# A short first load from adjacent rows, both first loads ahead of the barrier, and a transposed store

## The chip, the cores and the metric

One core of one Trainium2 chip; the other cores are idle. The metric is the device time of one execution in microseconds. The span of a profile runs from the first to the last instruction of the kernel and is some 1.3 us shorter. Where engines start, land or carry packets, the 16 DMA engines are meant.

## The reference

```python
x = np.random.randn(32, 512, 1024).astype(np.float32)   # 67.1 MB
relu_x = np.maximum(x, 0)
return np.sum(relu_x, axis=-1)                           # 32 x 512 sums
```

## The kernel before

The 16384 rows are dealt to 128 partitions. Region 0 gives each partition 112 neighbouring rows, region 1 gives it 16. Region 0 is loaded in seven chunks of 16 rows (64 KB per partition, one packet each; 16 DMA engines with 8 packets each) into three buffers; region 1 in ever smaller pieces, so that little work is left after the last landing. ScalarE takes the ReLU, VectorE the sums. SyncE issues all transfers. The first load's instruction is moved ahead of the barrier with which all engines open the program.

```python
REGIONS = [112, 16]
CHUNKS = [(0, 0), (0, 16), (0, 32), (0, 48), (0, 64), (0, 80), (0, 96)]
TAIL = [8, 4, 2, 1]
LAST = [512, 256, 256]
# ... views, buffers, semaphores cut ...
    for c in range(NBIG + 1):
        if c >= NB:
            sp.wait_ge(s_dve, done[c - NB])        # the buffer is free
        if c < NBIG:
            g, j = CHUNKS[c]
            sp.dma_start(out=buf[:, c % NB, :, :], in_=xv[g][:, j : j + BIG, :]).then_inc(
                s_in[c], 16
            )
        if c == 0:
            code.insert(arrival, code.pop())       # ahead of the barrier
# ... tail loads cut ...
    sp.wait_ge(s_fact, 1)
    sp.wait_ge(s_fdve, 1)
    for g in range(len(REGIONS) - 1):              # sums of region 0
        sp.dma_start(out=ov[g][:, :], in_=res[:, start[g] : start[g] + REGIONS[g]]
        ).then_inc(s_store, 16)
# ... ReLU on ScalarE, sums on VectorE, per chunk, cut ...
    sp.wait_ge(s_tdve, 1)
    sp.dma_start(out=ov[-1][:, :], in_=res[:, start[-1] : J]).then_inc(s_out, 16)
    sp.wait_ge(s_store, 16 * (len(REGIONS) - 1))
    sp.wait_ge(s_out, 16)
```

## Time and profile before

| | before |
|---|---|
| time, median of 3 runs | 161.12 us (161.08 to 161.19) |
| span of the profiled run | 159.8 us |
| first chunk taken up by ScalarE | 21.84 us |
| distance of the later chunks | 19.36 us (433 GB/s) |
| from the last load's landing to the end | 2.0 us |

How to read it: the time that ScalarE's first instruction of a chunk starts is the landing of that chunk plus 0.02 us, as long as "DMA" stands behind its idle time. A chunk has landed when the slowest of the 16 engines has landed its eight packets. So these few starts show the whole flow: the first one the start, their distances the rate. The lines are in the prediction below.

### The profile page before, as it was taken

The page shows a single profiled execution, that of the slowest core. Times are in us where ns is not written, and L with a number is a line of the kernel's source. Part 1 is how long each engine was busy: PE and PEld are TensorE (multiplying, and loading weights), DVE is VectorE, ACT ScalarE, POOL GpSimd, SP SyncE. Part 2 cuts the span into 40 slices and gives each one's busy share as a digit, 9 for nine tenths or more (in the row PEclk, how much of TensorE's full clock was granted, in tenths as well). Part 3 has the DMA queues.
Part 4 walks back from the last instruction along what each step waited for, and adds up shares of the span by engine and source line. Part 5 has one row for each costly group of instructions (what it writes and reads, how often), then busy time and mean ns, then how long its engine had stood idle before and what let it go on. Part 6 is the DMA issues. An engine that isn't in the chain of part 4 may idle for free.

```text
span 159.8 us, 148 instructions
## 1 busy us (share of the span) xinstructions
DVE 121.4 (76%) x58; ACT 101.5 (63%) x55; POOL 0.2 (0%) x4
## 2 busy tenths in 40 slices
DVE  0000000999959999999969989699899999598995
ACT  3000059990699808996099951999339980496974
POOL 0000000000000000000000000000000000000000
DMA  7996996996997998989969969969969969899994
GB/s 262 525 525 262 525 525 262 525 525 262 525 443 344 525 410 377 525 361 427 525 295 492 525 279 509 525 262 525 525 262 525 525 262 525 353 435 394 406 393 138
DMA packets 2305, 67.18 MB, mean 420 GB/s; under 512 B 512, under 2 KB 768, under 8 KB 1024
## 3 DMA queue, kind: packets, MB, share of 16 engines
q1 hardware_dynamic: 2304, 67.18, 98.0%
q14 instruction: 1, 0.01, 0.0%
HBM read 67.11 MB, written 0.07 MB: 420 GB/s over the span
## 4 chain that ended last, share of the span: by engine, by line
DMA 68%; ACT 18%; DVE 11%; SPq 1%; issue 0%
DMA buf<-in_x_dram 68%; ACT buf L130 18%; DVE res L145 11%; SPq L92 1%; SPq L100 0%; DVE buf L115 0%; DVE last L115 0%
## 5 line engine op out<-in xcount | busy, mean ns | idle before, releaser
L145 DVE TENSOR_REDUCE res<-buf 128x7 f32<-128x7168 f32 (+4 forms) x17 | 100.1, 5923 | 34.0 <-ACT buf L130 34.0
L130 ACT ACTIVATE buf<-buf 128x7168 f32<-128x7168 f32 (+4 forms) x16 | 80.7, 5099 | 46.5 <-DMA buf<-in_x_dram 46.5
L112 ACT ACTIVATE buf<-buf 128x1024 f32<-128x1024 f32 (+1 forms) x19 | 19.0, 1000 | 9.0 <-DMA buf<-in_x_dram 8.9
L115 DVE TENSOR_SCALAR_CACHE_REDUCE buf<-buf 128x1024 f32<-128x1024 f32 (+2 forms) x19 | 20.9, 1146 | 2.8 <-DMA buf<-in_x_dram 2.5
L112 ACT ACTIVATION_READ_ACCUMULATOR buf<-buf 128x1 f32 x19 | 3.5, 186 | 0.0
L130 ACT ACT_TABLE_LOAD x1 | 1.3, 1283 | 0.8 <-PEq L206 0.8
L115 DVE DVE_READ_ACCUMULATOR buf<-buf 128x1 f32 x19 | 1.6, 83 | 0.0
L115 DVE TENSOR_SCALAR_CACHE_REDUCE last<-last 128x258 f32<-128x258 f32 x1 | 0.4, 422 | 0.0
L175 DVE TENSOR_TENSOR res<-half 128x1 f32<-128x1 f32 x1 | 0.2, 160 | 0.1
L206 POOL MEMSET const-bfloat16-1.0<- 128x1 bf16 x1 | 0.1, 101 | 0.0
L206 POOL MEMSET const-uint8-127<- 128x1 uint8 x1 | 0.1, 101 | 0.0
L206 POOL MEMSET const-float32-0.0<- 128x1 f32 x1 | 0.1, 98 | 0.2 <-issue 0.2
L206 POOL MEMSET const-float32-1.0<- 128x1 f32 x1 | 0.1, 98 | 0.0
L115 DVE DVE_READ_ACCUMULATOR last<-last 128x1 f32 x1 | 0.1, 81 | 0.0
## 6 DMA issues: line engine op xcount, KB each, us to landing
buf<-in_x_dram SPq DMA_DIRECT2D x1, 4096.0 KB, 26.7
buf<-in_x_dram SPq DMA_DIRECT2D x1, 2048.0 KB, 31.2
buf<-in_x_dram SPq DMA_DIRECT2D x1, 1024.0 KB, 33.2
buf<-in_x_dram SPq DMA_DIRECT2D x1, 512.0 KB, 34.0
buf<-in_x_dram SPq DMA_DIRECT2D x1, 256.0 KB, 34.2
buf<-in_x_dram SPq DMA_DIRECT2D x1, 128.0 KB, 34.1
last<-in_x_dram SPq DMA_DIRECT2D x1, 128.0 KB, 34.0
buf<-in_x_dram SPq DMA_DIRECT2D x7, 36.3
```

What stands on the lines that cost most here:

```text
L92: sp.dma_start(out=buf[:, tb, r : r + n, :], in_=xv[-1][:, r : r + n, :]).then_inc(s_in[NBIG + i], 16)
L112: return act.activation(t, t, AF.Relu, accum_out=acc)
L115: return dve.tensor_scalar(out=t, in0=t, scalar1=0.0, scalar2=None, op0=ALU.max, op1=ALU.add, accum_out=acc)
L130: act.activation(t, t, AF.Relu).then_inc(s_act, 1)
L145: dve.tensor_reduce(out=res[:, c * BIG + r : c * BIG + r + n], in_=buf[:, c % NB, r : r + n, :], axis=X, op=ALU.add,).then_inc(s_dve, 1)
L175: dve.tensor_tensor(out=res[:, j0 + r : j0 + r + 1], in0=half[:, 0:1], in1=half[:, 1:2], op=ALU.add)
L206: nc = _bacc.Bacc("TRN2", target_bir_lowering=False, num_devices=1)
```

## The change

Intent: let the engines get going on short packets (4 KB) from 128 adjacent rows before they turn to packets of 60 KB, with both parts of the first chunk issued at once, and so begin the flow earlier. The row of the first region has one sum per partition. To store 128 sums of 4 bytes as four pieces of 128 bytes, VectorE transposes 32 x 32 blocks of them.

```diff
-REGIONS = [112, 16]
-CHUNKS = [(0, 0), (0, 16), (0, 32), (0, 48), (0, 64), (0, 80), (0, 96)]
+REGIONS = [1, 111, 16]
+CHUNKS = [[(0, 0, 1), (1, 0, 15)]] + [[(1, 16 * c + 15, 16)] for c in range(6)]
-DVE_STEPS = [[7, 9], [7, 4, 5], ...cut
+DVE_STEPS = [[7, 9], [7, 9], ...cut
@@ loads
-            g, j = CHUNKS[c]
-            sp.dma_start(out=buf[:, c % NB, :, :], in_=xv[g][:, j : j + BIG, :]).then_inc(s_in[c], 16)
-        if c == 0:
-            code.insert(arrival, code.pop())
+            i = 0
+            for g, j, n in CHUNKS[c]:
+                sp.dma_start(
+                    out=buf[:, c % NB, i : i + n, :], in_=xv[g][:, j : j + n, :]
+                ).then_inc(s_in[c], 16)
+                i += n
+                if c == 0:
+                    code.insert(arrival, code.pop())
+                    arrival += 1
@@ stores
-    for g in range(len(REGIONS) - 1): ...cut
+    sp.dma_start(out=ov[1][:, :], in_=res[:, start[1] : start[2]]).then_inc(s_store, 16)
+    sp.wait_ge(s_turn, 1)
+    sp.dma_start(
+        out=of[0:P].rearrange("(k q) -> k q", q=32), in_=turned[0:P:32, 0:32]
+    ).then_inc(s_store, 16)
@@ waits of ScalarE and VectorE
-        act.wait_ge(s_in[c], 16)
+        act.wait_ge(s_in[c], 16 * len(CHUNKS[c]))
@@ VectorE, behind the sums of chunk 1
+        if c == 1:
+            dve.wait_ge(s_dve, done[c])
+            dve.transpose(out=turned[:, :], in_=res[:, 0:32]).then_inc(s_turn, 1)
```

More of the change, by code (lines that the diff above doesn't have):

```diff
@@ L7 @@
 NB = 3
-REGIONS = [112, 16]
-CHUNKS = [(0, 0), (0, 16), (0, 32), (0, 48), (0, 64), (0, 80), (0, 96)]
+REGIONS = [1, 111, 16]
+CHUNKS = [[(0, 0, 1), (1, 0, 15)]] + [[(1, 16 * c + 15, 16)] for c in range(6)]
 ACT_STEPS = [[7, 9], [7, 9], [4, 5, 7], [4, 5, 7], [4, 5, 7], [3, 4, 5]]
-DVE_STEPS = [[7, 9], [7, 4, 5], [4, 5, 7], [4, 5, 7], [4, 5, 7], [3, 4, 5]]
+DVE_STEPS = [[7, 9], [7, 9], [4, 5, 7], [4, 5, 7], [4, 5, 7], [3, 4, 5]]
 TAIL = [8, 4, 2, 1]
@@ L50, in bass_relu_sum_kernel @@
     res = nc.alloc_sbuf_tensor("res", [P, J], fp32)
+    turned = nc.alloc_sbuf_tensor("turned", [P, 32], fp32)
     n_in = NBIG + len(TAIL) + len(LAST)
@@ L60, in bass_relu_sum_kernel @@
     s_tdve = nc.alloc_semaphore("s_tdve")
+    s_turn = nc.alloc_semaphore("s_turn")
     s_store = nc.alloc_semaphore("s_store")
@@ L82, in bass_relu_sum_kernel @@
         if c < NBIG:
-            g, j = CHUNKS[c]
-            sp.dma_start(out=buf[:, c % NB, :, :], in_=xv[g][:, j : j + BIG, :]).then_inc(
-                s_in[c], 16
-            )
-        if c == 0:
-            code.insert(arrival, code.pop())
+            i = 0
[7 more added lines that the diff above has]
+                    arrival += 1
     r = 0
@@ L104, in bass_relu_sum_kernel @@
     sp.wait_ge(s_fdve, 1)
-    for g in range(len(REGIONS) - 1):
-        sp.dma_start(
-            out=ov[g][:, :], in_=res[:, start[g] : start[g] + REGIONS[g]]
-        ).then_inc(s_store, 16)
+    sp.dma_start(out=ov[1][:, :], in_=res[:, start[1] : start[2]]).then_inc(s_store, 16)
[3 more added lines that the diff above has]
+    ).then_inc(s_store, 16)
     def on_act(t, acc):
@@ L136, in bass_relu_sum_kernel @@
         if alone:
-            dve.wait_ge(s_in[c], 16)
+            dve.wait_ge(s_in[c], 16 * len(CHUNKS[c]))
             for i in range(BIG - alone, BIG - alone // 2):
@@ L151, in bass_relu_sum_kernel @@
             r += n
+        if c == 1:
+            dve.wait_ge(s_dve, done[c])
+            dve.transpose(out=turned[:, :], in_=res[:, 0:32]).then_inc(s_turn, 1)
     j0 = NBIG * BIG
     for c in range(NTWO, NBIG):
-        act.wait_ge(s_in[c], 16)
-        dve.wait_ge(s_in[c], 16)
+        act.wait_ge(s_in[c], 16 * len(CHUNKS[c]))
+        dve.wait_ge(s_in[c], 16 * len(CHUNKS[c]))
         for i in range(BIG):
```

## The prediction

> **What bounds the kernel now.** I read the page first for the busy shares and the packets, then the timeline for the moments at which loads land, then windows over the first microseconds, because the change touches little but the start, and last the chain and the wait list for the end.
>
> ```profile
> span 159.8 us, 148 instructions
> DVE 121.4 (76%) x58; ACT 101.5 (63%) x55; POOL 0.2 (0%) x4
> ...
> q1 hardware_dynamic: 2304, 67.18, 98.0%
> ```
>
> The load queue is busy for 98% of what 16 engines have in the span; VectorE (76%) and ScalarE (63%) both have room. The timeline, columns start, length, engine, line, operation, with the idle time before it in brackets, says the same about ScalarE, which takes each chunk when it lands:
>
> ```profile
> 0.79 1.28 ACT L130 ACT_TABLE_LOAD   x1 [0.79 <-PEq L206]
> 21.84 13.95 ACT L130 ACTIVATE buf<-buf 128x7168 f32<-128x7168 f32 x2 [19.77 <-DMA buf<-in_x_dram]
> ...
> 41.20 13.95 ACT L130 ACTIVATE buf<-buf 128x7168 f32<-128x7168 f32 x2 [5.41 <-DMA buf<-in_x_dram]
> ...
> 118.60 10.63 ACT L130 ACTIVATE buf<-buf 128x3072 f32<-128x3072 f32 x3 [5.31 <-DMA buf<-in_x_dram]
> ...
> 137.96 1.06 ACT L112 ACTIVATE buf<-buf 128x1024 f32<-128x1024 f32 x1 [6.65 <-DMA buf<-in_x_dram]
> ...
> 147.66 1.06 ACT L112 ACTIVATE buf<-buf 128x1024 f32<-128x1024 f32 x1 [1.28 <-DMA buf<-in_x_dram]
> ```
>
> Chunks arrive every 41.20 - 21.84 = 19.36 us, from the second to the seventh alike (118.60 to 137.96 is 19.36 again). A chunk is 16 rows of 128 x 4 KB = 8.389 MB, so the flow is 433 GB/s. The first tail piece, 8 rows, takes 147.66 - 137.96 = 9.70 us, 1.21 us per row, and 19.36 / 16 is 1.21 too. The input is 128 such rows: 128 x 1.21 = 154.9 us of the 159.8 us. What is left is a start of some 21.84 - 19.36 = 2.48 us, from the first issue to the moment from which the flow counts (its landing latency included), and an end of some 2 us after the last landing. So only about 4.5 us of the span can be touched at all without a faster flow, and 2% of the time would be 3.2 us.
>
> The windows split the start. Columns: window, length, busy times of three engines, clock, DMA share, GB/s. A packet counts in the window in which it starts, with its whole length and size, so shares over 1 are no error.
>
> ```profile
> 0.00:1.00 1.00, 0.00 (x0) 0.21 (x1) 0.20 (x4) 1.00 0.00 0
> 1.00:2.00 1.00, 0.00 (x0) 1.00 (x1) 0.00 (x0) 1.00 3.09 1049
> 2.00:3.00 1.00, 0.00 (x0) 0.07 (x1) 0.00 (x0) 1.00 0.00 0
> 3.00:4.00 1.00, 0.00 (x0) 0.00 (x0) 0.00 (x0) 1.00 0.00 0
> 4.00:5.00 1.00, 0.00 (x0) 0.00 (x0) 0.00 (x0) 1.00 2.42 1049
> ```
>
> 1049 GB/s for 1 us is 16 packets of 64 KB, one per engine. The first 16 begin between 1 and 2 us and last 3.09 us on average; the second 16 last 2.42 us, which is the pace of the whole stream (65,536 B in 2.42 us is 27.1 GB/s, times 16 again 433). So the first packet of each engine costs 0.67 us more than later ones. Narrower windows:
>
> ```profile
> 1.00:1.10 0.10, 0.00 (x0) 0.10 (x1) 0.00 (x0) 1.00 14.33 4588
> ...
> 1.70:1.90 0.20, 0.00 (x0) 0.20 (x1) 0.00 (x0) 1.00 0.82 328
> ...
> 4.06:4.25 0.19, 0.00 (x0) 0.00 (x0) 0.00 (x0) 1.00 4.75 2059
> 4.25:4.40 0.15, 0.00 (x0) 0.00 (x0) 0.00 (x0) 1.00 4.03 1748
> 4.40:4.53 0.13, 0.00 (x0) 0.00 (x0) 0.00 (x0) 1.00 6.98 3025
> ```
>
> 4588 x 0.10 / 65.5 is 7 engines that begin in the first tenth; one begins only after 1.70. The share of the early seven is 14.33 x 0.10 x 16 / 7 = 3.28 us each, that of the late one 0.82 x 0.20 x 16 = 2.62. The engines that began first thus paid 0.86 us extra, the one that began last 0.20. The second packets start between 4.06 and 4.53; less 2.42 this is an "effective start" of 1.64 for the best engine and 2.11 for the worst. All engines carry equal bytes, so the worst one ends the stream.
>
> **What the Trainium skill says.** (1) "Perfetto Trace Analysis", section on the HWDGE DMA instruction: the profiled time of an issue leaves out the data movement, and an engine may begin before all descriptors are made. The trace agrees: the first issue is at 0.00, data begins 1.00 us later. (2) "DMA: Bandwidth & Descriptors", "Where 436 GB/s comes from": a ceiling of 435.2 GB/s at the SBUF ports. The trace has 433, so the flow itself has nothing to give. (3) The same page, "Latency and other measured facts", on HBM row pitch: large power-of-two pitches between partitions lose bandwidth, with streams in lock step as an unverified reason. Here the pitch is 112 x 4 KB = 448 KB; the steady stream loses nothing by it, and only the slow first packets would fit. (4) "VectorE: DVE Perf Modes", "The three transpose paths": VectorE transposes separate 32x32 blocks, 311 ns for 128x128 in bf16. No transpose is in the trace before.
>
> **The change part by part.**
>
> *The first load in two.* Row 0 of each partition now comes from 128 adjacent rows (512 KB in one piece), then 15 rows at a pitch of 111 x 4 KB = 444 KB. Removed: the first 64 KB packet on scattered addresses, all engines at once. Each engine instead starts with 8 packets of 4 KB, close together. If the extra 0.67 us is the engines getting in each other's way on far-apart addresses, the worst effective start falls from 2.11 towards the bound that the late engine shows (it began after 1.70 and paid 0.20: about 2.0), or towards 1.2 to 1.5 for early engines, if the late ones were late for the same reason. I take 1.75, a gain of 0.36 us; it is my choice between 2.0 and 1.5. Added: one more transfer boundary per engine. From the landings, 19.36 against 8 x 2.415 of data is 0.04 us per boundary; short packets add about as much again (4 KB in eight packets against one of 32 KB), so 0.08 us. Net -0.28 us.
>
> *Both loads ahead of the barrier.* An issue takes some 0.4 us, so SyncE comes to the barrier about 0.4 us later and ACT_TABLE_LOAD moves from 0.79 to about 1.2. ScalarE then idles 19.77 us before its first work: 0 on the path. Loads two and three are issued 0.4 us later, twenty and forty microseconds ahead of need: 0. The 15-row issue comes 0.4 us after the first, which holds 8 x 0.15 = 1.2 us of work per engine: no hole. ScalarE still waits for both parts, so no computing starts earlier.
>
> *VectorE.* In chunk 1 the 4-row and 5-row sums (4.42 + 5.48 us by the rows of section 5) become one of 9 rows (9.75): -0.15 us. The wait on itself and one transpose add an estimated 0.3 us. Chunk 1 ends at 65.0, and the load that waits for it is queued behind one that lands at 79.9: 15 us of slack, 0 on the path.
>
> *The stores.* One more issue (0.35 us) at about 147.6, four packets of 128 B, behind the loads. The first store is issued at 147.26 and lands 10.7 us later, 157.96; the last one goes out at 158.33 and lands 1.4 us later. Loads were all issued by 124.2. So the added store is finished with the first one: 0.
>
> Sum: 161.12 - 0.36 + 0.08 = 160.84; rounded, 160.8 us.
>
> **The rivals.** *The start is bound by the arming of the rings.* Then the late engine starts as late as now, the slowest effective start stays about 2.0 to 2.1, the boundary eats the rest: 161.1 to 161.2. For it: the engine that began last paid almost nothing extra and was still among the slow ones. Against: the early ones lost most, so something shared held them. *The 444 KB pitch slows the flow.* Each 1% of the 135 us of region 1 would be 1.3 us. Against it: 448 KB (chunks) and 64 KB (tail, 1.21 us per row) run at the same pace, set at the engines. It would need over 2% to matter. *The late barrier or the added store is on the path:* +0.4 us, 161.5. Against it are the 19.77 us of idle time and the store's slack. *A larger gain:* all engines at full pace from 1.2 us, 0.9 us less 0.08: 160.3. That would also need the late engines to start early.
>
> **Range and chances.** The range runs from most of the larger gain (160.3) to slightly above no gain at all (161.25). Beyond 2% on the fast side would need 3.2 us where the start has only about 2.5 us in all, 1.0 of it before any data: 1%. On the slow side only a worse flow could do it: 1%. Within 2%: 98%.
>
> **What would show it.** Right: first packets of 4 KB from about 1.0 us; 60 KB packets at the old 27.1 GB/s; the second chunk (now landing as a whole) some 0.3 us earlier than 41.18, and every later landing shifted by the same; the end after the last landing unchanged at 2 us. Wrong: landings at the old times (ring arming), landings spaced by more than 19.36 us (pitch), or a last store that waits for the transposed one.

## More of the kernel before

All runs told here were with a granted clock of 1.00. Runs of one session share one chip; sessions fell on different chips.

## The result, and the profile after

Time after: 161.14 us median of 6 runs (160.90 to 161.36); before, beside it, 161.14 (161.08 to 161.23). The ratio is 0.9999, with a 95% interval of 0.9986 to 1.0012: the same. A ratio here is the mean time of one kernel's fast runs over the mean of the other's of the same rounds, so not quite the ratio of the medians. The six runs are not one heap: in order they are 161.27, 161.31, 161.36, then 160.90, 161.01, 160.91. The profile is of the first, one of the slower ones.

The windows over the start of the changed kernel (columns as in the prediction):

```profile
1.00:2.00 1.00, 0.00 (x0) 0.73 (x1) 0.00 (x0) 1.00 0.91 229
2.00:3.00 1.00, 0.00 (x0) 0.55 (x1) 0.00 (x0) 1.00 2.95 1217
3.00:4.00 1.00, 0.00 (x0) 0.00 (x0) 0.00 (x0) 1.00 0.14 61
```

In the second microsecond 229 GB/s x 1 us / 4 KB = 56 short packets start, where the kernel before started 16 long ones; by 3 us most of the 60 KB packets have begun, and the last one begins after 3.00 (61 KB is one such packet; the trace's packet records, which hold the start, length and size of each packet but not its engine, say 3.01). Eight short packets at the stream's pace are 8 x 4096 B / 27.1 GB/s = 1.21 us, so the worst effective start is 3.01 - 1.21 = 1.80 us with the extra boundary in it. Before it was 2.11.

ScalarE's first instruction of each chunk, changed kernel, first profile:

```profile
21.65 13.95 ACT L137 ACTIVATE buf<-buf 128x7168 f32<-128x7168 f32 x2 [19.10 <-DMA buf<-in_x_dram]
...
60.36 14.04 ACT L137 ACTIVATE buf<-buf 128x4096 f32<-128x4096 f32 x3 [5.41 <-DMA buf<-in_x_dram]
79.80 14.04 ACT L137 ACTIVATE buf<-buf 128x4096 f32<-128x4096 f32 x3 [5.40 <-DMA buf<-in_x_dram]
...
118.50 10.63 ACT L137 ACTIVATE buf<-buf 128x3072 f32<-128x3072 f32 x3 [5.35 <-DMA buf<-in_x_dram]
137.96 1.06 ACT L119 ACTIVATE buf<-buf 128x1024 f32<-128x1024 f32 x1 [6.75 <-DMA buf<-in_x_dram]
...
155.02 1.06 ACT L119 ACTIVATE buf<-buf 128x1024 f32<-128x1024 f32 x1 [0.30 <-DMA buf<-in_x_dram]
156.51 0.63 ACT L119 ACTIVATE buf<-buf 128x512 f32<-128x512 f32 x1 [0.35 <-DMA buf<-in_x_dram]
```

The reader is to see a lead that is won and lost. The first chunk is there 0.19 us earlier than before (21.84). From 60.36 to 79.80 are 19.44 us and from 118.50 to 137.96 are 19.46, not 19.36, and 137.96 is the very time of before. The one-row piece of the tail then takes 156.51 - 155.02 = 1.49 us; landing to landing it took 1.29 before. The packet records show what happened: between 23 and 118 us, 64 packets of 64 KB last over 2.43 us (up to 2.66), where before only 8 do; together they are 2.7 us of engine time too long, and one engine's delay is enough to delay a chunk.

The other parts lie beside the path. The transpose and its store:

```profile
64.77 0.21 DVE L161 STREAM_TRANSPOSE turned<-res 128x32 f32<-128x32 f32 x1
...
147.65 0.63 SPq L113 DMA_DIRECT2D out_dram<-turned  x1
```

and in the wait list of SyncE's queue the last wait, for the last store, is as long as before; before, then after:

```profile
SPq L192 <- DMA out_dram<-res: 1.1, 1, 1.1
SPq L202 <- DMA out_dram<-res: 1.1, 1, 1.1
```

### The profile page after: what moved, and what is told of

It is laid out like the page before. It is cut to its first block, busy times and chain, and to the rows that moved or that the text cites. A ratio compares the mean times of both kernels' runs of the same rounds, so it can differ in the third digit from the quotient of the medians.

```text
span 159.9 us, 150 instructions
## 1 busy us (share of the span) xinstructions
DVE 121.5 (76%) x58; ACT 101.4 (63%) x55; POOL 0.2 (0%) x4
## 4 chain that ended last, share of the span: by engine, by line
DMA 68%; ACT 18%; DVE 11%; SPq 1%; issue 0%
DMA buf<-in_x_dram 68%; ACT buf L137 18%; DVE res L152 11%; SPq L98 1%; SPq L106 0%; DVE buf L122 0%; DVE last L122 0%
```

## The experiments

Theory at the outset: the short first packets start the flow 0.2 us earlier, and what loses it later has nothing to do with the change's addresses (L). Rival P: the new pitch of 444 KB between partitions makes packets slow. Twelve runs followed: the kernel before and the changed kernel again, and seven variants. In the table, "first landing" is the slowest engine's last packet of chunk 1 with its confirmation; "mean" and "last" are when the engines began their first packet of chunk 2, on average and the last of them; "too long" is the engine time lost to 64 KB packets of over 2.43 us between 23 and 118 us. All from the packet records of the one profiled run, whose own time stands beside it; what is said of a single engine is inferred from which packet begins where another ends.

| kernel | first landing | mean | last | too long | profiled run | median (lowest to highest) |
|---|---|---|---|---|---|---|
| before | 21.82 | 21.24 | 21.44 | 0.2 | 161.15 | 161.12 (161.08 to 161.19) |
| before2 | 21.87 | 21.31 | 21.52 | 0.1 | 161.19 | 161.17 (161.11 to 161.36) |
| changed | 21.62 | 21.10 | 21.31 | 2.7 | 161.27 | 161.14 (160.90 to 161.36) |
| again | 21.63 | 21.02 | 21.31 | 0.7 | 160.93 | 160.91 (160.89 to 161.01) |
| again2 | 21.56 | 20.98 | 21.27 | 0.9 | 160.95 | 161.01 (160.95 to 161.43) |
| contig448 | 21.69 | 21.06 | 21.35 | 3.1 | 161.12 | 161.06 (161.00 to 161.12) |
| split448 | 21.91 | 21.00 | 21.55 | 0.3 | 161.20 | 161.04 (160.87 to 162.01) |
| split448b | 21.76 | 21.07 | 21.41 | 2.2 | 161.14 | 161.25 (161.14 to 161.36) |
| pitch444 | 22.28 | 21.34 | 21.93 | 0.5 | 161.60 | 161.60 (161.51 to 161.72) |
| onebar | 21.88 | 21.09 | 21.54 | 0.2 | 161.24 | 162.36 (161.24 to 163.37) |
| onebar2 | 22.75 | 21.32 | 22.38 | 0.7 | 161.94 | 162.62 (161.94 to 163.30) |
| split448_onebar | 22.12 | 21.19 | 21.79 | 3.8 | 161.52 | 161.22 (160.98 to 161.52) |
| plain | 21.61 | 21.03 | 21.28 | 0.7 | 165.03 | 165.04 (164.88 to 165.76) |
| plain_early | 21.61 | 21.00 | 21.29 | 89 | 167.22 | 166.79 (166.77 to 167.22) |

### again and again2: the changed kernel unaltered

> The changed kernel, unaltered, a third time. In its first profile the first chunk landed at 21.62 us instead of 21.82, and the lead of 0.20 us was gone by 137.93 us, through load packets of 2.43 to 2.66 us that lay scattered between 76 and 123 us where the kernel before has steady ones of 2.42. Its six runs fell in two groups, 161.27 to 161.36 and 160.90 to 161.01. Theory P (the new pitch of 444 KB makes packets slow): slow packets again, the second to seventh landings more than 19.36 us apart on average, about 161.1 or more. Theory L (luck of the run or of the chip): the lead may be kept here, then 160.9 us, with landings 19.36 apart. Both: first landing at about 21.62.

Measured: ratio 0.9985 to the kernel before (0.9972 to 0.9998). The chunks, by ScalarE's first instructions:

```profile
21.65 13.95 ACT L137 ACTIVATE buf<-buf 128x7168 f32<-128x7168 f32 x2 [19.10 <-DMA buf<-in_x_dram]
...
79.70 14.04 ACT L137 ACTIVATE buf<-buf 128x4096 f32<-128x4096 f32 x3 [5.29 <-DMA buf<-in_x_dram]
...
118.41 10.63 ACT L137 ACTIVATE buf<-buf 128x3072 f32<-128x3072 f32 x3 [5.31 <-DMA buf<-in_x_dram]
137.77 1.06 ACT L119 ACTIVATE buf<-buf 128x1024 f32<-128x1024 f32 x1 [6.65 <-DMA buf<-in_x_dram]
```

The start is that of the first profile to 0.01 us, the distances are 19.35 on average ((137.77 - 21.65) / 6), and the lead of 0.19 is still there at 137.77. The same program at the same pitch thus keeps its lead here: theory P in its plain form falls.

> The changed kernel once more, in another session. So far its first chunk landed at 21.62 us both times; in one session the lead of 0.2 us was lost to slow packets between 76 and 123 us (161.3 us), in the other it was kept (160.91 us). Theory L (the slow packets come with the session or the chip, not with the kernel's pitch) expects either about 160.9 or about 161.3, all five runs within 0.15 us of each other; the first landing 21.6 to 21.7 in any case. Theory P, that the pitch costs time whenever it is used, has already met one session against it and would need 161.1 or more here.

Measured, on another chip: ratio 0.9989 (0.9977 to 1.0000), the first landing as expected. But one of the five runs took 161.43 us, so the loss can come within a session too; my word that all five would lie within 0.15 us was wrong. Over the result and these two sessions, the changed kernel's 16 runs average 161.05 us and the 28 runs of the kernel before 161.21: 0.16 us, 0.1%.

### before2: the kernel before against itself

> The kernel before against itself, for the size of the noise and for a second trace. Ratio 1.000 within 0.0007. First landing 21.8 within 0.1; landings 19.35 apart; the engines about 0.46 us apart from first to last packet of a round, if this spread belongs to the kernel; anything from 0.4 to 0.9 if it is chance.

Measured: ratio 0.9996 (0.9984 to 1.0008), first landing 21.87. The engines' spread at the start of chunk 2 was 0.42 us, near the 0.46 of the first trace. The noise of such a comparison is thus about 0.1%, the size of the effect itself; the landings in the traces separate the kernels better than the times do.

### contig448: the adjacent row at the old pitch

Its output is wrong, which doesn't matter for the time. The short load takes rows 0 to 127, the other loads are those of the old layout.

```diff
-REGIONS = [1, 111, 16]
-CHUNKS = [[(0, 0, 1), (1, 0, 15)]] + [[(1, 16 * c + 15, 16)] for c in range(6)]
+REGIONS = [112, 16]
+CHUNKS = [[(0, 0, 1), (0, 1, 15)]] + [[(0, 16 * c, 16)] for c in range(1, 7)]
+                if n == 1:
+                    src = xr[0:P, :].rearrange("(p j) d -> p j d", p=P)
```

> Wrong result on purpose: the first short load takes the 128 adjacent rows at the front of the input, the other 15 rows and all chunks keep the old pitch of 448 KB. Traffic is the same in size and number. Theory P: first landing near 21.62, landings 19.36 apart to the end, 160.9 us. Theory L: the same start, but slow packets may appear here as well, and the time can be anything from 160.9 to 161.3.

Measured: ratio 0.9993 (0.9981 to 1.0005). The start is as with the change (21.69), and in this trace 49 packets are too long, by 3.1 us in all, mostly between 50 and 80 us, at the pitch of 448 KB. This is the other half of the case against P: slow packets come at the old pitch as well (also in split448b and split448_onebar).

### split448 and split448b: the split alone

```diff
-CHUNKS = [(0, 0), (0, 16), (0, 32), ...cut
+CHUNKS = [[(0, 0, 1), (0, 1, 15)]] + [[(0, 16 * c, 16)] for c in range(1, 7)]
```

with the loop of the change, both loads ahead of the barrier, and the old store.

> Only the split: row 0 then rows 1 to 15 of each partition, both ahead of the barrier, at the old pitch of 448 KB, no transposed store. If short first packets are all that the start needs: first landing near 21.62 and, without the 444 KB pitch, the lead of 0.20 kept to the end under theory P, so about 160.9 us. If the rows must be adjacent in memory for the start to gain, the first landing stays at 21.8 or comes later by the extra boundary of 0.08 us, and the time is 161.1 to 161.2.

Measured: ratio 1.0001 (0.9983 to 1.0019), first landing 21.91. The starts of chunk 2's packets, in three windows, of this kernel and then of the changed one (run again):

```profile
20.70:21.20 0.50, 0.00 (x0) 0.00 (x0) 0.00 (x0) 1.00 4.25 1835
21.20:21.45 0.25, 0.00 (x0) 0.00 (x0) 0.00 (x0) 1.00 0.60 262
21.45:21.60 0.15, 0.00 (x0) 0.00 (x0) 0.00 (x0) 1.00 1.01 437
```

```profile
20.70:21.20 0.50, 0.00 (x0) 0.00 (x0) 0.00 (x0) 1.00 4.56 1966
21.20:21.45 0.25, 0.00 (x0) 0.00 (x0) 0.00 (x0) 1.00 0.61 262
21.45:21.60 0.15, 0.00 (x0) 0.00 (x0) 0.00 (x0) 1.00 0.00 0
```

By rate x length / 65,536 B: 14, 1 and 1 engines against 15, 1 and none. The average engine is as early as with the change (21.00), but one engine is late, and the slowest one counts. The packet records show why: it stalled for 0.68 us in one 4 KB packet (0.16 as a rule). In the first profile of the changed kernel three 4 KB packets take 0.66 us, but on engines that had begun by 1.1 us, and no engine comes to its first long packet later than 3.01 us (here 3.44).

> The split at the old pitch, both loads ahead of the barrier, a second time. If adjacent first rows keep the engines together and scattered ones don't, the engines are again 0.8 us apart from first to last packet of a round and the first landing is at 21.8 to 21.9; with adjacent rows four traces show 0.39 to 0.55 and 21.56 to 21.69. If the late engine of the first run was chance: 0.5 us apart, first landing 21.6 to 21.7, 160.9 us.

Measured: ratio 1.0005 (0.9987 to 1.0024), first landing 21.76, spread 0.64 us: between the two expectations. Six traces with adjacent rows and both loads ahead have first landings of 21.56 to 21.69, the two with scattered rows 21.76 and 21.91. The short packets move the average engine, the adjacent rows keep the slowest one with it; with two traces on one side the second half is likely rather than shown.

### pitch444: the long load first

```diff
-            i = 0
-            for g, j, n in CHUNKS[c]:
+            for g, j, n in CHUNKS[c][::-1]:      # 15 rows, then the adjacent row
+                i = 1 if c == 0 and g == 1 else 0
# ... the issue, as it was, cut ...
-                i += n
```

> The changed kernel with the two first loads in the other order: 15 rows at the 444 KB pitch first, the adjacent row second; stores as in the change. The start should be that of the kernel before (first packets of 60 KB about 0.67 us too long), first landing about 21.85 to 21.9. Theory P: slow packets later too, so 161.3 us or more. Theory L: 161.15 to 161.25, the boundary of 0.04 to 0.08 us added to the time of before.

Measured: 161.60 us, ratio 1.0028 (1.0016 to 1.0040), slower than both of my expectations. Not by slow packets later: these are few (0.5 us). The start itself is bad. In chunk 2 the average engine starts at 21.34, 0.10 after that of before, as expected; but two engines begin their second packet 0.4 us after all others and stay behind, so that the first landing is 22.28. The theories had no term for this. What it shows safely is that the order matters: with everything else of the change in place, a long first packet gives 161.60, a short one 160.91 on the same chip.

### onebar, onebar2 and split448_onebar: only the row ahead of the barrier

```diff
-                if c == 0:
+                if c == 0 and n == 1:
                     code.insert(arrival, code.pop())
```

> The changed kernel with only the one-row load ahead of the opening barrier and the 15-row load behind it (issued about 0.4 us later). If both loads ahead matter to the flow, engines run dry between the row and the rest: the first row lasts until about 2.7 us and the second issue would come at about 0.85 us, so I expect no hole, a first landing as with the change, 21.6 us, and 160.9 us. If the second issue, close behind the first, disturbs the start of some engines, this one starts better than the change, 21.5 us.

Measured: median 162.36 us, ratio 1.0067 (1.0037 to 1.0096); only the profiled run took 161.24, the others 162.25 to 163.37. I had expected no loss. A second profile was to catch a slow run:

> The kernel with only the one-row load ahead of the barrier, a second time, to catch the slow executions (162.3 to 163.4 us, five of six) in a trace; the traced one took 161.24. Theory H (the engines run dry): the 15-row load is issued late, or its packets begin later than the 2.7 us at which the row's packets end, and every later landing is late by about 1.2 us, the first at about 22.9 us. Theory S (something later): first landing near 21.9, and the microsecond is lost in the stream or the end.

Measured: 161.94 profiled, 163.30 in the other run; ratio 1.0090 (1.0048 to 1.0132). Windows around the moment at which the row's packets end, for this run and then for the changed kernel (again2):

```profile
2.90:3.10 0.20, 0.00 (x0) 0.00 (x0) 0.00 (x0) 1.00 0.71 307
3.10:3.60 0.50, 0.00 (x0) 0.00 (x0) 0.00 (x0) 1.00 0.00 0
3.60:3.90 0.30, 0.00 (x0) 0.00 (x0) 0.00 (x0) 1.00 1.15 410
```

```profile
2.90:3.10 0.20, 0.00 (x0) 0.00 (x0) 0.00 (x0) 1.00 0.73 307
3.10:3.60 0.50, 0.00 (x0) 0.00 (x0) 0.00 (x0) 1.00 0.00 0
3.60:3.90 0.30, 0.00 (x0) 0.00 (x0) 0.00 (x0) 1.00 0.00 0
```

In the changed kernel nothing starts after 3.10, since every engine is at its first long packet. In onebar2, 410 x 0.30 / 61.4 KB is two packets that start between 3.60 and 3.90, at 3.69 and 3.81 by the records, 0.66 us and more after the row had ended on every engine (3.03). Having run dry, they pay the start again: 1.15 x 0.30 x 16 / 2 = 2.76 us each instead of 2.27. The load had been issued at 0.80 us, 2.2 us before the row had ended everywhere; the first issue of the program shows data after 1.0. This is theory H, in two engines of 16, and the whole flow is late for it:

```profile
22.77 13.95 ACT L137 ACTIVATE buf<-buf 128x7168 f32<-128x7168 f32 x2 [20.70 <-DMA buf<-in_x_dram]
```

1.1 us after the changed kernel's 21.65. So putting both loads ahead of the barrier is not a detail: the row covers only 1.2 us of work per engine. With the issue at 0.45 us none of the traces here in which the row comes first has such a hole; with 0.80, one of the two traces of this kernel has. Runs of 163.3 are not covered by this trace; a longer hole is likely but not shown. Why these two engines got their packets so late is open.

> Row 0 and rows 1 to 15 at the old pitch, the second load behind the barrier; no adjacent rows and no transposed store. In the first split run the mean start of the engines was as good as with the change, but one engine stalled 0.5 us in a 4 KB packet and set the end. If that was chance, this gives a first landing of 21.6 to 21.7 and 160.9 to 161.0 us, as good as the change with neither adjacent rows nor the transpose. If adjacent rows keep single engines from stalling, one engine is late again: landing at 21.8 to 21.9 and about 161.1.

Measured: ratio 0.9995 (0.9982 to 1.0008), three runs at 160.98 to 161.09 and three at 161.35 to 161.52, the profiled one among the slower. Its engines are 0.86 us apart. A scattered row with the second load behind the barrier is at times as fast as the change and at times not; why it was spared the hole of onebar2, with its second issue as late (0.79 us), stays open.

### plain: the sums stored without the transpose

```diff
-    sp.wait_ge(s_turn, 1)
-    sp.dma_start(out=of[0:P].rearrange("(k q) -> k q", q=32), in_=turned[0:P:32, 0:32]).then_inc(s_store, 16)
+    sp.dma_start(out=ov[0][:, :], in_=res[:, 0:1]).then_inc(s_store, 16)
```

and no transpose on VectorE.

> The changed kernel without the transpose: the sums of the first row are stored straight from their column, 4 bytes to each of 128 addresses, by an issue right behind the 55.5 KB store at 147.3 us. My theory: the store is off the path whatever its shape, since both stores queue behind the loads and are done at about 158.0 to 158.3, before the last store lands at 159.5. Time as with the change, 160.9 to 161.0 us, ratio to before 0.9985 to 0.9990. Rival (the transpose is there for a reason): 128 single 4-byte writes take so long that the wait for both stores ends after the last store; then 161.2 us or more, and the end of the span would be released by that store.

Measured: 165.04 us, ratio 1.0259 (1.0235 to 1.0282). My theory fell by 4 us. The issues with size and time to landing, and SyncE's last wait:

```profile
out_dram<-res SPq DMA_DIRECT2D x1, 55.5 KB, 10.6
out_dram<-res SPq DMA_DIRECT2D x1, 0.5 KB, 15.3
out_dram<-res SPq DMA_DIRECT2D x1, 8.0 KB, 4.9
```

```profile
SPq L196 <- DMA out_dram<-res: 4.5, 1, 4.5
```

The 0.5 KB of sums, issued at 147.58, is confirmed at 162.9, and the last store, whose 8 KB took 1.4 us before, takes 4.9: it lands behind them, at 163.1. The packets of the small store show as 9 ns each on the engines, and all have started by 157.3 us; the time is in the confirmations, which come one after the other, the last at 162.9 us.

### plain_early: the same store, hidden early

```diff
+        if c == NB:
+            sp.dma_start(out=ov[0][:, :], in_=res[:, 0:1]).then_inc(s_store, 16)
```

behind the fourth chunk's load, instead of at the end.

> The changed kernel without the transpose, its 128 sums of 4 bytes stored early: issued behind the fourth chunk's load at about 45.6 us, so that the store's packets come after that load, at about 79.7 us, and are confirmed long before the end. Theory W (each 4-byte write is cheap for the engine but slow to be confirmed; at the end this held up the last store until 163.1 us): here the confirmation is hidden, 160.9 to 161.05 us, as with the transposed store, so neither transpose nor extra wait is needed. Rival: the unconfirmed writes hold up the load packets behind them as well, the landing after 79.7 comes up to 5 us late, and the time is 164 to 166 us.

Measured: 166.79 us, ratio 1.0344 (1.0330 to 1.0358). The rival was right. ScalarE's chunks around the store:

```profile
79.98 14.04 ACT L135 ACTIVATE buf<-buf 128x4096 f32<-128x4096 f32 x3 [5.46 <-DMA buf<-in_x_dram]
...
105.06 14.04 ACT L135 ACTIVATE buf<-buf 128x4096 f32<-128x4096 f32 x3 [11.04 <-DMA buf<-in_x_dram]
```

The 9 us after the store, here and then in the kernel before:

```profile
79.00:88.00 9.00, 7.55 (x3) 8.02 (x3) 0.00 (x0) 1.00 1.14 233
79.00:88.00 9.00, 7.70 (x3) 8.11 (x3) 0.00 (x0) 1.00 1.06 459
```

The chunk behind the store comes after 25.08 us instead of 19.36: 5.7 us are lost, and in the 9 us after the store began the flow is 233 GB/s; the kernel before has 459 in the same window. Load packets of 64 KB behind the store last up to 7.95 us. So this store of 128 writes of 4 bytes costs 4 us at the end and 5.7 us of the whole flow in the middle; in the one place tried it was not hidden behind the loads of its queue. The transpose, 0.21 us of VectorE off the path, is what makes the one-row region affordable here. The 128 sums lie side by side, in one stretch of 512 bytes: whether 4-byte writes to places far apart cost as much was not tried, nor was another queue for the store.

## Why the prediction was right or wrong

**The bound and the limits**: right. The flow is 19.36 us per chunk in every kernel that isn't disturbed; only the start could move, and the time stayed within 2% and within the range. The range (160.3 to 161.25) held the time of before too, so the 161.14 alone says nothing for the gain of 0.28 us, which the first six runs do not show (ratio 0.9999). What speaks for the mechanism is the landings.

**The start**: the step is right and nearly right in size; its reason is so in part. The step "I take 1.75", with 0.08 for the boundary, makes 1.83 for the worst engine; measured 1.80 in the first profile. Of the 0.28 us net, 0.20 were left at the first landing of the first profile and 0.22 to 0.24 on average (21.56 to 21.63 in the three traces of the changed kernel against 21.82 and 21.87). The mis-sized term is the 0.08 us for the boundary. The boundary itself costs about 0.01 us by the packet records, but the sign "60 KB packets at the old 27.1 GB/s" was not quite met: the first round of them lasts 2.32 us instead of 2.27, and in the seven rounds behind it 8, 24 and 26 packets of the three traces are too long (by over 0.012 us, as in the table). Together that is 0.11 to 0.16 us per engine by the end of the first chunk, where 0.08 was put. The gain at the first landing did not come from the adjacent rows alone, as the reason in the prediction had it: scattered short packets move the average engine just as far (21.00 and 21.07 against 20.98 to 21.10). Why a short first packet pays less of the extra than a long one is not shown.

**"Every later landing shifted by the same"**: this is the step that failed in the first profile. The lead was gone when ScalarE took the tail at 137.96 us. In the other two profiles it held (landings at 137.74 and 137.79 against 137.94 and 137.96) and those times, 160.91 and 161.01, are close to the 160.84 predicted. The sum had no term for stray slow packets. The rival of the slow pitch is not the cause: the lead is kept at 444 KB and such packets come at 448. What sets them off is open. In the first chunk they go with the short start in every trace: in rounds two to eight of its long packets the three traces that begin with long ones (before, before2, pitch444) have none, none and one that is too long, and the eleven that begin with short ones 4 to 37. The pitch and the adjacent rows are no part of it, since pitch444 has both and one such packet, and split448 has neither and four. Later, between 23 and 118 us, the two groups overlap (0.1 to 0.5 us of engine time against 0.2 to 3.8, leaving out plain_early), so a tie of the late ones to the short start is possible, not shown.

**"Both loads ahead of the barrier"**: 0 on the path, as said, but for too little reason. The prediction asked only what the later barrier costs, and took the second issue's own delay to be that of the first, so the row's 1.2 us seemed ample. With the second load behind the barrier (onebar, onebar2) the median rose to 162.36 and 162.62 us: in the one slow run with a trace, two engines stood idle for 0.66 us and more before they began the second load.

**The stores**: 0, as said, for the transposed one (its issue took 0.63 us where 0.35 was assumed, off the path). "Finished with the first one" is close: the two stores were confirmed at 158.5 in the first profile, 157.7 in the second. But the step saw nothing of why the transpose was there; the plain form costs 4 to 5.7 us.

**VectorE**: the 9-row sum took 9.75 us and the transpose 0.21 (estimated 0.3), with the slack as described: right.

**The rivals**: a start bound by the arming of the rings is not what the traces show. The second trace of the kernel before (before2) tells most: all 16 first packets begin by 1.50 us (below; 2097 GB/s x 0.50 us / 65,536 B = 16), where in the first trace the last began at 1.86, and the first landing is no earlier for it, 21.87. The later barrier and the added store are off the path.

```profile
1.00:1.50 0.50, 0.00 (x0) 0.50 (x1) 0.00 (x0) 1.00 6.55 2097
```

## What to carry to other kernels

When one queue runs at its ceiling, look at the slowest of its engines in the first microseconds: a short first packet brings the flow forward by about 0.2 us here, provided that the next load is issued early enough that no engine runs dry. Such a lead is no larger than what one slow packet can take (2.66 us instead of 2.42), so judge it by landings in several traces, not by one median. And before a layout leaves one number per partition to be stored, count the writes: 128 of 4 bytes, side by side, cost 4 to 5.7 us here, some twenty times what the change can win and more.

## What the Trainium skill lacked or had wrong

- "DMA: Bandwidth & Descriptors", section "Specifications", gives 512 B as the least transfer for line rate, below which there is a read-modify-write. It has no size of the loss for single words: 128 writes of 4 B took 5.7 us out of the flow and kept the loads behind them waiting, while 128 of 444 B and 128 of 64 B, also under 512 B, landed in the usual time (the 64 B ones 1.4 us after their issue). In these runs the loss shows at 4 B and not at 64 B; nothing between was tried.
- The same page, "Latency and other measured facts", gives about 0.6 us to the first byte for these issues. It does not say from which moment. Here the first data comes 1.00 us after the start of the first issue and 0.62 us after its end (at 0.38), so the figure fits if it counts from the end. It gives no spread: in one trace two engines of 16 stood idle for 0.66 us and more with the second load issued 2.2 us before.
- The same section's entry on row pitch has no figure for a pitch below 512 KB: 444 KB, 448 KB and (tail) 64 KB between partitions all ran at 1.21 us per row of 128 x 4 KB; no loss at any of them in the steady stream.
- No page that I read says that engines keep the offset with which they start: in the kernel before it is 0.46 us in the second round and 0.40 at 117.7 us. In split448 the engine that was late at the start still sets the landing at 138.01 (137.94 before), with few slow packets between (0.3 us of engine time).
